# Expert blocks of 1024 columns, with tiles of the two experts in groups of four

## The chip, the cores and the metric

The kernel runs on one core of one Trainium2 chip. The core has a matrix engine (TensorE, PE in the rows, with its weight loads as PEld), a vector engine (VectorE, DVE), a scalar engine (ScalarE, ACT), GpSimd (POOL), and a synchronisation engine (SyncE, SP) that issues nearly all transfers here. Data comes from HBM by 16 DMA engines into SBUF; matrix products land in PSUM, which has eight banks of 512 float32 columns per partition. The metric is device time in microseconds, the median of three runs; a profile is one execution of the same program.

## The reference

Two decoder layers over 256 tokens of width 1024, all in float32. Each has a mixing part and a channel part. The channel part of layer 0 is a dense SwiGLU; that of layer 1, about which this document is, sends each token to two of eight experts:

```python
def _swiglu(x, w1, w3, w2):
    return (jax.nn.silu(x @ w1) * (x @ w3)) @ w2

logits = (xt @ w_router).astype(jnp.float32)
top_v, top_e = lax.top_k(logits, TOP_K)          # 2 of 8
gates = jax.nn.softmax(top_v, axis=-1)
...
y = jnp.zeros((T, D), x.dtype).at[stok].add(yb[dest] * sg[:, None].astype(x.dtype))
```

An expert has `w1` and `w3` of 1024 x 3584 and `w2` of 3584 x 1024, 44 MB of float32 in the three. All eight are read: 352 MB.

## The kernel before

Products in float32 are made from parts. ScalarE rounds a weight tile to a high part (`whi`, `cast_hi`, L1133), VectorE subtracts it from the raw tile to get the low part (`wlo`, `cast_lo`, L1141), and TensorE multiplies the parts in its fast format.

**Pairs of experts.** Experts are ranked by their load and worked on in four pairs. The first of a pair (role 0, "large" here) has up to 128 tokens, and each of its products takes three matmuls (`mm3`, L119 to L121). The second (role 1, "small") has at most 64 tokens, so that the high and the low parts of its tokens lie side by side in one stationary operand, and two matmuls do (`two`, L1080 and L1081); the halves are added later. Tokens are gathered by a matmul with a selection matrix (`select`, `gather`), one eighth of the width at a time, into `g`.

**Tiles and steps.** Work goes in steps, one for each weight tile of 1 MB (128 partitions x 2048 float32). `plan` lists them. The hidden width of 3584 is cut into blocks of `BN` = 512 columns, seven for each expert. A block has four up steps, two for `w1` and two for `w3`, each of four chunks of 128 rows by 512 columns; a row piece that the DMA reads is 2 KB. Then come the down steps of the block two before (the same expert's one before): two tiles of `w2`, each of two chunks of 128 rows with the full width of 1024, 4 KB in a row. Blocks of the two experts alternate, so that six steps of the large one are followed by six of the small one. A pair has 84 steps, the stage 336.

**What a block's result goes through.** The sums of a block gather in a PSUM bank (`mps`), one for `w1` and one for `w3`. For a large block `gated` takes the silu on ScalarE and `product` (L1258) multiplies on VectorE into `mh`; four transposes (`turn_pe`, `htp`, L1271) turn it, and `turn_large` splits it into `hi` and `lo`. For a small block `lift` (L1250) copies both sums to SBUF, matmuls with `fold` turn them and add the halves (`ftp`, L1267), and `turn_silu`, `turn_mult` (`fs`), `turn_small` (`sh`) follow. Down steps accumulate in two banks of each expert (`macc`). After an expert's last down step `sel_t` turns its selection matrix, `acc_split` splits its sum into `yh` and `yl`, and `combine` adds it to the tokens in four parts (`cbp`, then an add on VectorE into `x`, L1319).

**What sets the order.** `run` writes the order of every engine out by hand: at step s it first does what is noted in `mid[s]`, then casts the high part of step s + `ah` and the low part of step s + `al` (one less than the buffers of each, so both 4), asks for one more raw tile, does the step's matmuls, and then what is noted in `end[s]`. SP issues one transfer for each raw tile (`fetch`, L95) as soon as its buffer, one of six, is free: that is after the subtraction of the tile that held it. There are five buffers of high parts and five of low parts. PSUM has four banks for `mps`, `htp`, `ftp`, `gps`, `stp` and `cbp` together (`mmp`), and four for `macc`.

```python
        for s, (kind, bi, mat, k0) in enumerate(steps):
            for f in mid[s]:
                f()
            self.cast_hi(s + ah)
            self.cast_lo(s + al)
            self.more()
```

## Time and profile before

| | |
|---|---|
| median of three runs | 1692.51 us (1691.47 to 1692.65) |
| the profiled execution's own time | 1691.51 us |
| its span, first to last instruction | 1689.7 us |
| share of the span busy: TensorE, VectorE, ScalarE, GpSimd | 96%, 82%, 68%, 3% |
| transfers of expert weights | 336 of 1024 KB, median 11.5 us from issue to landing |

The first of the 336 transfers is issued at 755.31 us, so the last 55% of the span is the expert stage. Busy shares are averages over stages that differ; a matmul's busy time overlaps the next one's. Idle time is put down to the semaphore that came last.

### The profile page before, as it was taken

The page shows a single profiled execution, that of the slowest core. Times are in us where ns is not written, and L with a number is a line of the kernel's source. Part 1 is how long each engine was busy: PE and PEld are TensorE (multiplying, and loading weights), DVE is VectorE, ACT ScalarE, POOL GpSimd, SP SyncE. Part 2 cuts the span into 40 slices and gives each one's busy share as a digit, 9 for nine tenths or more (in the row PEclk, how much of TensorE's full clock was granted, in tenths as well). Part 3 has the DMA queues.
Part 4 walks back from the last instruction along what each step waited for, and adds up shares of the span by engine and source line. Part 5 has one row for each costly group of instructions (what it writes and reads, how often), then busy time and mean ns, then how long its engine had stood idle before and what let it go on. Part 6 is the DMA issues. An engine that isn't in the chain of part 4 may idle for free.

```text
span 1689.7 us, 22227 instructions
## 1 busy us (share of the span) xinstructions
PE 1625.3 (96%) x8152; PEld 1341.3 (79%) x8152; DVE 1386.1 (82%) x1686; ACT 1145.0 (68%) x1366; POOL 44.4 (3%) x40
## 2 busy tenths in 40 slices
PE   8899999999989999999999999999999999999996
PEld 7788787888878887877887787877878878778774
DVE  6987786554567667869999999999999998899987
ACT  5546744443436667448888888788887888778874
POOL 0331000000000000000000000000000000000000
PEclk9999999999999999999999999999999999999998
DMA  7534365555546443629999999999999999999993
GB/s 250 167 125 138 132 207 182 197 186 175 193 124 213 132 156 132 211 93 381 395 392 395 394 392 394 394 393 395 393 392 392 392 395 394 394 391 393 395 395 129
DMA packets 220733, 481.23 MB, mean 285 GB/s; under 512 B 8876, under 2 KB 33592, under 8 KB 220616
## 3 DMA queue, kind: packets, MB, share of 16 engines
q1 hardware_dynamic: 219272, 474.98, 77.3%
q0 software_dynamic: 1344, 4.75, 0.9%
q8 instruction: 66, 1.08, 0.3%
q14 instruction: 51, 0.42, 0.1%
HBM read 478.65 MB, written 1.05 MB: 284 GB/s over the span
## 4 chain that ended last, share of the span: by engine, by line
DMA 28%; DVE 15%; PE 6%; ACT 6%; issue 5%; ACTq 0%; DVEq 0%
DMA raw<-in_expert_w_dram 28%; DVE wlo L1141 11%; ACT whi L1133 5%; DVE x L1319 1%; PE plps L119 0%; PE plps L120 0%; PE plps L121 0%; PE bap L121 0%; PE bap L120 0%; PE yo L121 0%; PE bap L119 0%; PE yo L119 0%; PE yo L120 0%; DVE yl L128 0%; DVE mh L1258 0%
## 5 line engine op out<-in xcount | busy, mean ns | idle before, releaser
L1141 DVE TENSOR_TENSOR wlo<-raw,whi 128x2048 fp32r<-128x2048 f32 (+1 forms) x338 | 763.7, 2274 | 61.9 <-ACT whi L1133 59.9
L1133 ACT CAST whi<-raw 128x2048 fp32r<-128x2048 f32 (+1 forms) x338 | 641.3, 1902 | 152.9 <-DMA raw<-in_expert_w_dram 143.9
L107 DVE TENSOR_TENSOR wlo<-raw,whi 128x1024 fp32r<-128x1024 f32 (+2 forms) x218 | 254.7, 1190 | 148.1 <-issue 78.2
L105 ACT CAST whi<-raw 128x1024 fp32r<-128x1024 f32 (+2 forms) x222 | 218.5, 1016 | 177.5 <-PE hps L121 51.7
L119 PE MATMUL mps<-wlo,g 128*128 128x512 f32 x448 | 179.2, 400 | 1.8 <-DVE fs L1280 1.8
L1080 PE MATMUL mps<-wlo,g 128*128 128x512 f32 x448 | 179.8, 401 | 0.0
L1081 PE MATMUL mps<-whi,g 128*128 128x512 f32 x448 | 176.8, 395 | 0.0
L121 PE MATMUL mps<-whi,g 128*128 128x512 f32 x448 | 176.5, 394 | 0.0
L120 PE MATMUL mps<-whi,g 128*128 128x512 f32 x448 | 176.0, 393 | 0.0
L119 PEld LDWEIGHTS mps<-wlo,g 128*128 128x128 f32 x448 | 84.3, 188 | 20.5 <-DVE fs L1280 2.8
L121 PEld LDWEIGHTS mps<-whi,g 128*128 128x128 f32 x448 | 84.1, 188 | 19.4
L1080 PEld LDWEIGHTS mps<-wlo,g 128*128 128x128 f32 x448 | 84.8, 189 | 18.0
L1081 PEld LDWEIGHTS mps<-whi,g 128*128 128x128 f32 x448 | 84.9, 190 | 17.7
L120 PEld LDWEIGHTS mps<-whi,g 128*128 128x128 f32 x448 | 84.3, 188 | 17.9
L402 PE MATMUL dqp<-x,whi 128*128 128x512 f32 x256 | 95.5, 413 | 2.2 <-DVE vm L486 2.2
L1080 PE MATMUL macc<-wlo,sh 128*128 128x512 f32 x224 | 90.1, 402 | 3.0 <-DVE wlo L1141 1.8
L119 PE MATMUL macc<-wlo,hi 128*128 128x512 f32 x224 | 88.6, 396 | 0.0
L121 PE MATMUL macc<-whi,lo 128*128 128x512 f32 x224 | 88.2, 394 | 0.0
L120 PE MATMUL macc<-whi,hi 128*128 128x512 f32 x224 | 88.0, 393 | 0.0
L1081 PE MATMUL macc<-whi,sh 128*128 128x512 f32 x224 | 87.9, 393 | 0.0
L119 PE MATMUL hps<-wlo,x 128*128 128x512 f32 (+1 forms) x192 | 71.8, 374 | 0.0
L121 PE MATMUL hps<-whi,x 128*128 128x512 f32 (+1 forms) x192 | 71.4, 372 | 0.0
(373 smaller groups left out, 2958.7 us busy)
## 6 DMA issues: line engine op xcount, KB each, us to landing
raw<-in_expert_w_dram SPq DMA_DIRECT2D x336, 1024.0 KB, 11.5
raw<-in_w_in_dram SPq DMA_DIRECT2D x40, 1024.0 KB, 5.1
raw<-in_dense_w_dram SPq DMA_DIRECT2D x33, 1024.0 KB, 5.1
raw<-in_w_branch_diff_dram SPq DMA_DIRECT2D x8, 1024.0 KB, 5.0
raw<-in_w_out_dram SPq DMA_DIRECT2D x8, 1024.0 KB, 5.0
raw<-in_w_ple_gate_dram SPq DMA_DIRECT2D x8, 1024.0 KB, 5.1
raw<-in_w_branch_mla_dram SPq DMA_DIRECT2D x4, 1024.0 KB, 5.1
raw<-in_w_in_dram SPq DMA_DIRECT2D x4, 768.0 KB, 4.8
```

The source lines that it names most:

```text
L105: self.latest = nc.scalar.copy(hi[:, s], raw[:, s])
L107: nc.vector.tensor_tensor(lo[:, s], raw[:, s], hi[:, s], op=OP.subtract)
L119: mm(ps, sh, ml, start=first, stop=False)
L120: mm(ps, sh, mh, start=False, stop=False)
L121: mm(ps, sl, mh, start=False, stop=last)
L402: mm(*one, start=k == 0 and m == 0, stop=end and m == 1)
L1080: mm(ps, st, ml, start=first, stop=False)
L1081: mm(ps, st, mh, start=False, stop=last)
L1133: self.nc.scalar.copy(hi[:, p], raw[:, p])
L1141: self.nc.vector.tensor_tensor(lo[:, p], raw[:, p], self.his[s][:, p], op=OP.subtract)
L1319: nc.vector.scalar_tensor_tensor(self.x[:, tb, cs], ps, gate, self.x[:, tb, cs], op0=OP.mult, op1=OP.add, **kw)
```

## The change

`BN` becomes 1024. An expert has three blocks of 1024 columns and one of 512. An up tile of a wide block has two chunks of 128 rows by 1024 columns, 4 KB in a row; one of the last block stays as it was. A wide block has eight up steps and four down steps. `plan` no longer alternates whole blocks: four tiles of `w1` of the large expert, four of the small one, four of `w3` of each, then the four down tiles of the small block before and the four of the large block before.

A wide block uses two PSUM banks for each of `w1` and `w3`. The turn of a wide large block stands three steps after its last up step (two before); the turn of a small block stands after the last down step of the small block before it. Gathers for the next pair stand beside down steps, one at a time but for the last two. The combine of a small expert stands at one step, that of a large one at four. The low parts have four buffers instead of five (`al` is 3), `mh` has four instead of three, and the selection matrix is kept for two pairs instead of four. The number of matmuls and of casts is the same.

```diff
@@ -40,9 +40,9 @@
 HI_BUFS, XHI_BUFS = 3, 2
-LO_BUFS, XLO_BUFS = 2, 3
-MH_BUFS = 3
-BN = 512
+LO_BUFS, XLO_BUFS = 2, 2
+MH_BUFS = 4
+BN = 1024
 LCAP, SCAP = 128, 64
...
@@ -1081,14 +1081,16 @@
         mm(ps, st, mh, start=False, stop=last)
 
     def plan(self, jobs):
-        lanes, n = min(2, len(jobs)), EF // BN
-        blocks = [(m + a, i) for m in range(0, len(jobs), lanes) for i in range(n) for a in range(lanes)]
+        lanes, cuts = min(2, len(jobs)), range(0, EF, BN)
+        blocks = [(m + a, c0, min(BN, EF - c0)) for m in range(0, len(jobs), lanes) for c0 in cuts for a in range(lanes)]
         steps = []
-        for b in range(len(blocks) + lanes):
-            if b < len(blocks):
-                steps += [("up", b, mat, k0) for mat in (0, 1) for k0 in range(0, KC, 4)]
-            if b >= lanes:
-                steps += [("down", b - lanes, 0, r) for r in range(0, BN // 128, 2)]
+        for b0 in range(0, len(blocks) + lanes, lanes):
+            for mat in (0, 1):
+                for b in range(b0, min(b0 + lanes, len(blocks))):
+                    steps += [("up", b, mat, k0) for k0 in range(0, KC, 2048 // blocks[b][2])]
+            late = list(range(max(0, b0 - lanes), b0))
+            for b in late if b0 >= len(blocks) else late[::-1]:
+                steps += [("down", b, 0, r) for r in range(0, blocks[b][2] // 128, 2)]
         return blocks, steps
...
@@ -1104,15 +1106,15 @@
         if kind == "up":
-            nm, r, nk, c0, n = ("expert_w1", "expert_w3")[mat], k0, 4, i * BN, BN
+            nm, r, nk = ("expert_w1", "expert_w3")[mat], k0, 2048 // n
         else:
-            nm, r, nk, c0, n = "expert_w2", i * (BN // 128) + k0, 2, 0, D
+            nm, r, nk, c0, n = "expert_w2", c0 // 128 + k0, 2, 0, D
         w = self.i[nm][self.j][bass.ds(self.expert[m], 1), r * 128:(r + nk) * 128, c0:c0 + n]
...
@@ -1155,29 +1157,35 @@
+        lanes = 2 if pairs else 1
...
+        def after(b0):
+            return last["up", b0 + lanes - 1, 1] + 1
+
         for q in order[1:]:
             m = [x for x, job in enumerate(jobs) if job[0] == q][0]
-            s0 = first["up", blocks.index((m - 2, EF // BN - 1)), 0]
-            mid[s0 - 8].append(lambda q=q: self.select(q))
-            mid[s0].append(lambda q=q: new_g(q))
-            for x, d in enumerate((0, 1, 2, 3, 6, 7, 8, 9)):
-                end[s0 + d].append(lambda q=q, x=x: self.gather(gs[q], q, (x,), wide, self.mmp, "mm"))
-
-        for bi, (m, i) in enumerate(blocks):
+            b0 = [x for x, blk in enumerate(blocks) if blk[0] == m - 2][2]
+            mid[first["up", b0, 0]].append(lambda q=q: self.select(q))
+            mid[after(b0)].append(lambda q=q: new_g(q))
+            for x, d in enumerate((0, 1, 2, 4, 5, 6, 7, 7)):
+                end[after(b0) + d].append(lambda q=q, x=x: self.gather(gs[q], q, (x,), wide, self.mmp, "mm"))
+
+        for bi, (m, c0, n) in enumerate(blocks):
             small = jobs[m][2]
             s1, s3 = last["up", bi, 0], last["up", bi, 1]
             if small:
                 for mat, s in ((0, s1), (1, s3)):
                     mid[s + 1].append(lambda bi=bi, mat=mat: self.lift(ups, hid, bi, mat))
+                t = last["down", bi - lanes, 0] if bi >= lanes else s3 + 2
             else:
                 mid[s1 + 1].append(lambda bi=bi: self.gated(ups, hid, bi))
                 mid[s3 + 1].append(lambda bi=bi: self.product(ups, hid, bi))
-            t = s3 + 2
+                t = s3 + n // 512 + (1 if n > 512 else 0)
             end[t].append(lambda bi=bi: self.turn_pe(hid, turn, bi))
...
@@ -1185,22 +1193,30 @@
-            if i == EF // BN - 1:
+            if c0 + n == EF:
                 d0, d1 = first["down", bi, 0], last["down", bi, 0]
-                over = m == len(jobs) - 1
-                near = m >= len(jobs) - 2
-                end[d0].append(lambda m=m: self.sel_t(accs, m))
-                if over:
+
+                def parts(*at):
+                    for part, s in enumerate(at):
+                        end[s].append(lambda m=m, part=part: self.combine(accs, m, (part,), None))
+
+                if m == len(jobs) - 1:
+                    end[d0].append(lambda m=m: self.sel_t(accs, m))
                     end[d1].append(lambda m=m: self.acc_split(accs, m))
                     end[d1].append(lambda m=m: self.combine(accs, m, range(4), done))
-                elif near:
+                elif m == len(jobs) - 2:
+                    end[d0].append(lambda m=m: self.sel_t(accs, m))
                     mid[d1 + 1].append(lambda m=m: self.acc_split(accs, m))
-                    end[d1 + 1].append(lambda m=m: self.combine(accs, m, range(4), None))
+                    parts(*[d1 + 1] * 4)
+                elif small:
+                    end[d0].append(lambda m=m: self.sel_t(accs, m))
+                    mid[d1 + 1].append(lambda m=m: self.acc_split(accs, m))
+                    parts(*[d1 + 2] * 4)
                 else:
-                    x, y = (d1 + 7, d1 + 13) if small else (d1 + 1, d1 + 7)
-                    mid[x].append(lambda m=m: self.acc_split(accs, m))
-                    for part in range(4):
-                        end[y + part].append(lambda m=m, part=part: self.combine(accs, m, (part,), None))
+                    z = after(bi + 4)
+                    end[z].append(lambda m=m: self.sel_t(accs, m))
+                    mid[z + 1].append(lambda m=m: self.acc_split(accs, m))
+                    parts(z + 2, z + 4, z + 5, z + 6)
...
@@ -1214,31 +1230,33 @@
             if kind == "up":
                 if k0 == 0:
-                    ups[bi, mat] = self.mmp.tile([128, 512], F32, name="mps", tag="mm")
-                for k in range(4):
-                    w = [t[:, k * BN:(k + 1) * BN] for t in (hi, lo)]
-                    ends = k0 + k == 0, k0 + k == KC - 1
-                    if small:
-                        self.two(ups[bi, mat], gs[q][:, k0 + k, 1], *w, *ends)
-                    else:
-                        self.mm3(ups[bi, mat], gs[q][:, k0 + k, 0], gs[q][:, k0 + k, 2], *w, *ends)
+                    ups[bi, mat] = [self.mmp.tile([128, 512], F32, name="mps", tag="mm") for _ in range(n // 512)]
+                for k in range(2048 // n):
...
@@ -1246,56 +1264,71 @@
...
     def gated(self, ups, hid, bi):
-        hid[bi] = h = self.hidden()
-        self.nc.scalar.activation(h, ups.pop((bi, 0)), AF.Silu)
+        hid[bi] = []
+        for ps in ups.pop((bi, 0)):
+            h = self.hidden()
+            self.nc.scalar.activation(h, ps, AF.Silu)
+            hid[bi].append(h)
 
     def product(self, ups, hid, bi):
-        self.nc.vector.tensor_tensor(hid[bi], hid[bi], ups.pop((bi, 1)), op=OP.mult)
+        for h, ps in zip(hid[bi], ups.pop((bi, 1))):
+            self.nc.vector.tensor_tensor(h, h, ps, op=OP.mult)
 
     def turn_pe(self, hid, turn, bi):
         nc = self.nc
+        small = self.jobs[self.blocks[bi][0]][2]
         hs = hid.pop(bi)
-        if self.jobs[self.blocks[bi][0]][2]:
-            ps = self.mmp.tile([128, 2, 4, SCAP], F32, name="ftp", tag="mm")
-            for a in range(2):
+        turn[bi] = {"ps": []}
+        for n in range(self.blocks[bi][2] // 512):
+            if small:
+                ps = self.mmp.tile([128, 2, 4, SCAP], F32, name="ftp", tag="mm")
+                for a in range(2):
+                    for q in range(4):
+                        nc.tensor.matmul(ps[:, a, q, :], hs[a][n][:, q * 128:(q + 1) * 128], self.fold, start=True, stop=True)
+            else:
+                ps = self.mmp.tile([128, 4, 128], F32, name="htp", tag="mm")
                 for q in range(4):
-                    nc.tensor.matmul(ps[:, a, q, :], hs[a][:, q * 128:(q + 1) * 128], self.fold, start=True, stop=True)
-        else:
-            ps = self.mmp.tile([128, 4, 128], F32, name="htp", tag="mm")
-            for q in range(4):
-                nc.tensor.transpose(ps[:, q, :], hs[:, q * 128:(q + 1) * 128], self.ident)
-        turn[bi] = {"ps": ps}
+                    nc.tensor.transpose(ps[:, q, :], hs[n][:, q * 128:(q + 1) * 128], self.ident)
+            turn[bi]["ps"].append(ps)
...
     def turn_large(self, turn, bi):
-        hh, hl = (self.mp.tile([128, 4, 128], F32R, name=nm) for nm in ("hi", "lo"))
-        self.split(hh, hl, turn[bi]["ps"])
+        hh, hl = (self.mp.tile([128, 2, 4, 128], F32R, name=nm, tag=nm, bufs=2) for nm in ("hi", "lo"))
+        for n, ps in enumerate(turn[bi]["ps"]):
+            self.split(hh[:, n], hl[:, n], ps)
         turn[bi] = {"st": (hh, hl)}
```

On VectorE, one round in the middle of the first pair, from one `product` (`mh<-mh,mps`) to the small split (`sh<-fs,sh`). Before, with its low parts (`wlo`) between:

```order
L1141 TENSOR_TENSOR wlo<-raw,whi 128x2048 x3
L1258 TENSOR_TENSOR mh<-mh,mps 128x512
L1141 TENSOR_TENSOR wlo<-raw,whi 128x2048 x2
L128 TENSOR_TENSOR lo<-htp,hi 128x512
L1141 TENSOR_TENSOR wlo<-raw,whi 128x2048 x6
L1280 TENSOR_TENSOR fs<-fs,ftp 128x256
L1141 TENSOR_TENSOR wlo<-raw,whi 128x2048
L128 TENSOR_TENSOR sh<-fs,sh 128x4x64
```

and now, on the same engine:

```order
L1143 TENSOR_TENSOR wlo<-raw,whi 128x2048 x9
L1283 TENSOR_TENSOR mh<-mh,mps 128x512 x2
L1143 TENSOR_TENSOR wlo<-raw,whi 128x2048 x3
L128 TENSOR_TENSOR lo<-htp,hi 128x512 x2
L1143 TENSOR_TENSOR wlo<-raw,whi 128x2048 x5
L1311 TENSOR_TENSOR fs<-fs,ftp 128x256 x2
L1143 TENSOR_TENSOR wlo<-raw,whi 128x2048
L128 TENSOR_TENSOR sh<-fs,sh 128x4x64 x2
```

The instructions between low parts now come by twos, half as often, and three low parts instead of two stand between a product and the split of its turned form.

On TensorE, the turn of a small block (`ftp`). Before, it stood between a small down tile (`macc<-whi,sh`) and the large expert's next up tile:

```order
L1080 MATMUL macc<-wlo,sh 128x512
L1081 MATMUL macc<-whi,sh 128x512
L1267 MATMUL ftp<-fold,mh 128x64 x8
L119 MATMUL mps<-wlo,g 128x512
L120 MATMUL mps<-whi,g 128x512
L121 MATMUL mps<-whi,g 128x512
```

and now it stands between the small and the large down tiles:

```order
L1080 MATMUL macc<-wlo,sh 128x512
L1081 MATMUL macc<-whi,sh 128x512
L1295 MATMUL ftp<-fold,mh 128x64 x16
L119 MATMUL macc<-wlo,hi 128x512
L120 MATMUL macc<-whi,hi 128x512
L121 MATMUL macc<-whi,lo 128x512
```

Two turns now stand together, and four large down tiles come behind them, with four large up tiles after those.

On TensorE, the turn of a large block (`htp`). Before, behind two large down tiles:

```order
L119 MATMUL macc<-wlo,hi 128x512
L120 MATMUL macc<-whi,hi 128x512
L121 MATMUL macc<-whi,lo 128x512
L1271 MATMUL htp<-ident,mh 128x128 x4
L1080 MATMUL mps<-wlo,g 128x512
L1081 MATMUL mps<-whi,g 128x512
```

and now behind the third small up tile:

```order
L1080 MATMUL mps<-wlo,g 128x512
L1081 MATMUL mps<-whi,g 128x512
L1299 MATMUL htp<-ident,mh 128x128 x8
L1080 MATMUL mps<-wlo,g 128x512
L1081 MATMUL mps<-whi,g 128x512
```

The two turns of a wide block stand inside a group of small up tiles, whose fourth tile follows them.

## Rows read from the trace of the kernel before

**Rows 1.** The page: busy time of each engine, and GB/s in 40 slices.

```profile
span 1689.7 us, 22227 instructions
...
PE 1625.3 (96%) x8152; PEld 1341.3 (79%) x8152; DVE 1386.1 (82%) x1686; ACT 1145.0 (68%) x1366; POOL 44.4 (3%) x40
...
GB/s 250 167 125 138 132 207 182 197 186 175 193 124 213 132 156 132 211 93 381 395 392 395 394 392 394 394 393 395 393 392 392 392 395 394 394 391 393 395 395 129
```

**Rows 2.** The page: the chain that ended last, by engine and by line.

```profile
DMA 28%; DVE 15%; PE 6%; ACT 6%; issue 5%; ACTq 0%; DVEq 0%
DMA raw<-in_expert_w_dram 28%; DVE wlo L1141 11%; ACT whi L1133 5%; DVE x L1319 1%; PE plps L119 0%; PE plps L120 0%; PE plps L121 0%; PE bap L121 0%; PE bap L120 0%; PE yo L121 0%; PE bap L119 0%; PE yo L119 0%; PE yo L120 0%; DVE yl L128 0%; DVE mh L1258 0%
```

**Rows 3.** Busy time by stretch: engines with counts, clock, DMA share, GB/s.

```profile
1084.00:1307.00 223.00, 218.47 (x1027) 178.43 (x1026) 209.00 (x128) 182.49 (x147) 0.00 (x0) 1.00 1.04 393
...
1020.00:1080.00 60.00, 58.54 (x267) 47.00 (x265) 58.68 (x41) 48.67 (x36) 0.00 (x0) 1.00 1.04 393
```

**Rows 4.** ScalarE in order of time: start, duration, casts that waited for a landing.

```profile
1105.53 1.92 ACT L1133 CAST whi<-raw 128x2048 fp32r<-128x2048 f32 x1 [0.33 <-DMA raw<-in_expert_w_dram]
...
1113.67 1.91 ACT L1133 CAST whi<-raw 128x2048 fp32r<-128x2048 f32 x1 [0.83 <-DMA raw<-in_expert_w_dram]
...
1118.87 1.91 ACT L1133 CAST whi<-raw 128x2048 fp32r<-128x2048 f32 x1 [0.19 <-DMA raw<-in_expert_w_dram]
...
1121.56 1.92 ACT L1133 CAST whi<-raw 128x2048 fp32r<-128x2048 f32 x1 [0.29 <-DMA raw<-in_expert_w_dram]
...
1129.55 1.91 ACT L1133 CAST whi<-raw 128x2048 fp32r<-128x2048 f32 x1 [0.70 <-DMA raw<-in_expert_w_dram]
...
1134.75 1.91 ACT L1133 CAST whi<-raw 128x2048 fp32r<-128x2048 f32 x1 [0.74 <-DMA raw<-in_expert_w_dram]
...
1137.43 1.90 ACT L1133 CAST whi<-raw 128x2048 fp32r<-128x2048 f32 x1 [0.29 <-DMA raw<-in_expert_w_dram]
```

**Rows 5.** Busy time by stretch: down tiles, up tiles, then down tiles alone.

```profile
1113.50:1118.60 5.10, 5.10 (x23) 4.12 (x23) 4.66 (x4) 4.42 (x4) 0.00 (x0) 1.00 1.03 398
1118.60:1129.30 10.70, 10.09 (x45) 7.90 (x44) 9.88 (x7) 8.21 (x6) 0.00 (x0) 1.00 1.05 391
...
1647.00:1655.00 8.00, 7.98 (x35) 6.19 (x34) 7.45 (x5) 6.94 (x6) 0.00 (x0) 1.00 1.03 410
```

**Rows 6.** The chain in order of time: start, duration, what.

```profile
1043.35 8.92 DMA raw<-in_expert_w_dram
...
1112.52 11.65 DMA raw<-in_expert_w_dram
...
1655.57 1.92 ACT whi L1133
```

**Rows 7.** The page: issues, count, KB of one, median us from issue to landing.

```profile
raw<-in_expert_w_dram SPq DMA_DIRECT2D x336, 1024.0 KB, 11.5
raw<-in_w_in_dram SPq DMA_DIRECT2D x40, 1024.0 KB, 5.1
```

**Rows 8.** Groups, 1084 to 1307 us: busy, mean ns, idle before and its end.

```profile
L1141 DVE TENSOR_TENSOR wlo<-raw,whi 128x2048 fp32r<-128x2048 f32 x84 | 190.9, 2286 | 14.5 <-ACT whi L1133 13.8 <-PE macc L1081 0.4
...
L119 PE MATMUL mps<-wlo,g 128*128 128x512 f32 x110 | 44.1, 401 | 0.8 <-DVE fs L1280 0.8
...
L1267 PE MATMUL ftp<-fold,mh 128*128 128x64 f32 x112 | 13.9, 273 | 1.1 <-ACT mh L1250 1.1
...
L1271 PE MATMUL htp<-ident,mh 128*128 128x128 f32 x28 | 4.4, 278 | 2.1 <-DVE mh L1258 2.0
```

**Rows 9.** TensorE in order of time: first starts of two blocks, a small turn.

```profile
772.57 0.41 PE L119 MATMUL mps<-wlo,g 128*128 128x512 f32 x1
...
783.64 0.39 PE L1080 MATMUL mps<-wlo,g 128*128 128x512 f32 x1
...
1013.26 1.89 PE L1267 MATMUL ftp<-fold,mh 128*128 128x64 f32 x16
1014.97 0.48 PE L119 MATMUL mps<-wlo,g 128*128 128x512 f32 x1
```

More of the change, by code (lines that the diff above doesn't have):

```diff
@@ L958, in before_moe @@
         self.places(cps, m, gg, eq)
-        self.sel = rp.tile([128, 2, NP, 256], F32R, name="sel", tag="sel")
+        self.sel = rp.tile([128, 2, 2, 256], F32R, name="sel")
         self.select(0)
@@ L1106, in more @@
         kind, bi, mat, k0 = self.steps[t]
[L1107 removed]
+        m, c0, n = self.blocks[bi]
         if m not in self.expert:
@@ L1216, in run @@
             self.more()
-            m, i = blocks[bi]
+            m, c0, n = blocks[bi]
             q, role, small = jobs[m]
@@ L1278, in turn_mult @@
+    def turn_silu(self, turn, bi):
+        turn[bi]["s"] = []
+        for ps in turn[bi]["ps"]:
+            s = self.mp.tile([128, 4, SCAP], F32, name="fs", bufs=2)
+            self.nc.scalar.activation(s, ps[:, 0], AF.Silu)
+            turn[bi]["s"].append(s)
     def turn_mult(self, turn, bi):
-        s = turn[bi]["s"]
-        self.nc.vector.tensor_tensor(s, s, turn[bi]["ps"][:, 1], op=OP.mult)
+        for s, ps in zip(turn[bi]["s"], turn[bi]["ps"]):
+            self.nc.vector.tensor_tensor(s, s, ps[:, 1], op=OP.mult)
@@ L1282, in turn_small @@
     def turn_small(self, turn, bi):
-        hh = self.mp.tile([128, 4, 128], F32R, name="sh")
-        self.split(hh[:, :, :SCAP], hh[:, :, SCAP:], turn[bi]["s"])
+        hh = self.mp.tile([128, 2, 4, 128], F32R, name="sh")
+        for n, s in enumerate(turn[bi]["s"]):
+            self.split(hh[:, n, :, :SCAP], hh[:, n, :, SCAP:], s)
         turn[bi] = {"st": (hh,)}
     def turn_large(self, turn, bi):
-        hh, hl = (self.mp.tile([128, 4, 128], F32R, name=nm) for nm in ("hi", "lo"))
-        self.split(hh, hl, turn[bi]["ps"])
+        hh, hl = (self.mp.tile([128, 2, 4, 128], F32R, name=nm, tag=nm, bufs=2) for nm in ("hi", "lo"))
@@ L1293, in sel_t @@
         q, _, small = self.jobs[m]
-        st = accs[m]["st"] = self.mp.tile([128, T], F32R, name="selt", bufs=2)
+        st = accs[m]["st"] = self.mp.tile([128, T], F32R, name="selt")
         ps = self.mmp.tile([128, 512], F32, name="stp", tag="mm")
```

38 lines of the change are left out of this document (23 added, 15 removed).

## The prediction

> **What bounds the kernel now.** The page's busy shares come first: TensorE 96% of the span, VectorE 82%, and a GB/s line that jumps from about 150 to 394 near slice 18 and stays there to the end [rows 1]. Shares over the span cannot say who ends last, so the chain of waits comes next. Its largest part by far is the transfer of expert weights, 28% of the span, ahead of the low-part subtraction on VectorE at 11% [rows 2]. One pair of experts is 84 tiles of 1 MB; the stretch from 1084 to 1307 us holds 84 subtractions [rows 8], so it is one pair's worth of work. In it the DMA moves 393 GB/s at a share of 1.04 while VectorE is busy 209.0 and ScalarE 182.5 of 223 us [rows 3]. TensorE looks full at 218.5, but a matmul's busy time overlaps the next one's, so I count it by starts further down. In the timeline of ScalarE, almost every cast starts when a tile lands [rows 4]: the queue is never empty and the engines wait for it. So the expert stage, which is where the whole change lies, lasts as long as its 336 tiles take to land.
>
> **What a row's width is worth.** A tile's cost can be read from the distance of two landings. Six tiles in the old order are four up tiles (rows of 2 KB) and two down tiles (rows of 4 KB). The cast that starts at 1105.53 is followed by the one six tiles later at 1121.56 and by the next at 1137.43: 16.03 and 15.87 us, 15.95 on the mean, 223.3 for 84 tiles [rows 4]. The two down tiles inside them take 1118.87 - 1113.67 = 5.20 and 1134.75 - 1129.55 = 5.20 us, 2.60 each [rows 4]; where only down tiles are left, from 1647 to 1655 us, the rate is 410 GB/s, or 1.0486 MB / 410 = 2.56 us each [rows 5]. The up tiles are what is left: (15.95 - 5.20) / 4 = 2.69 us, or 2.71 with 2.56 for a down tile. Short stretches say the same in GB/s: 398 over a stretch of down tiles, 391 over one of up tiles [rows 5].
>
> The change gives 4 KB rows to three of the three and a half blocks of each expert: 24 of its 28 up tiles, 192 of 224 in all; the last half block keeps 2 KB. Each gains between 2.69 - 2.60 = 0.09 and 2.71 - 2.56 = 0.15 us, so 192 tiles gain 17 to 29 us. I take 2.70 and 2.58, 0.12 us a tile, **-23 us**. The time of 84 tiles falls from 223.3 to 223.3 - 48 x 0.12 = 217.5 us.
>
> The Trainium skill (DMA: Bandwidth & Descriptors, Why small descriptors are slow) speaks for less: it gives a fixed overhead of about three cycles per packet beside 32-byte beats, so 2 x 67 = 134 cycles for two 2 KB packets and 131 for one of 4 KB, 2.2%, which would be 0.06 us a tile and 11.5 us in all, an estimate from that page. The trace, with 2.70 against 2.58, shows about twice that, and the measured landings decide the sum.
>
> **Who comes next.** TensorE: 48 matmuls of 512 columns start between 772.57 and 783.64 us, 0.2306 us each [rows 9]. A tile of the first expert (role 0, called large here) takes 12 of them, 2.77 us; of the second (small) 8, 1.84 us. A pair has 42 x 12 + 42 x 8 = 840, and 16 more combine results: 856 x 0.2306 = 197.4. To this come seven turns of small blocks at 1014.97 - 1013.26 = 1.71 us [rows 9], 12.0; seven turns of large ones, 4.4 at most [rows 8]; and 32 gather matmuls of 192 columns, 2.8 (an estimate by their columns from the same 0.2306). Together 216.6 us, against 217.5 for the new transfers. The change alters none of these counts. So the second bound stands 0.9 us behind the first, and every wait of TensorE that isn't already inside a wait for data now costs time. In the pair shown, the waits with a name are 0.8 for the small block's product, 1.1 for its lifted halves, and 2.1 for the product ahead of a large turn [rows 8]. If all 4.0 stayed, a pair would take 220.6 and the loss would be 4 x 3.1 = 12; if none did, 0. The causes of the last two are weakened: the rows of the order show that the turn of a large block now stands three small tiles behind the product instead of two tiles, the product stands behind the low parts of one tile fewer (three ahead instead of four, as there is one buffer less), and the small turn is now behind the four down tiles after its last lift, not two. So I take a value nearer to the lower end, **+5 us** (0 to 12).
>
> VectorE needs at most its 209.0 busy us of a pair [rows 3], 8.5 less than 217.5; its instructions are the same in number, and that margin hides the two adds or subtractions that now stand together, and the four adds of a combine at one step. ScalarE has 35 us to spare. The smaller selection table, the larger hidden tiles and the fewer descriptors cost nothing behind the same margins. The start of the stage is unchanged ahead of the first landing. After the last landing, 34.1 us pass (cast at 1655.57, end of the span 1689.7) [rows 1, 6]; the same steps stand there but for a small turn that moves ahead, 2 us at best, and TensorE may arrive 4 us later. I count **0** (-2 to +4).
>
> **Sum.** The profiled execution took 1691.5 by its own time, 1689.7 of it the span. 1691.5 - 23 + 5 + 0 = 1673.5. The median of the runs is 1.0 above that execution, so I forecast **1674.5 us**. Its own range, from the bounds, is 1692.5 - 29 - 2 = 1661.5 to 1692.5 - 17 + 12 + 4 = 1691.5; I hold 1666 to 1681 as its likely part.
>
> **Rivals.**
>
> *Half the gain, because rows are far apart.* A down tile is one contiguous megabyte, an up tile's rows lie 14,336 bytes apart (3584 columns of 4 bytes); no row of before shows wide rows with such gaps. If they land halfway, at 2.64 us, the gain is 11.5; 84 tiles then take 220.4, TensorE has 3.8 spare and the +5 goes away: 1692.5 - 11.5 = 1681. By the packet rule of the Trainium skill (DMA: Bandwidth & Descriptors, Why small descriptors are slow) the time would be the same.
>
> *TensorE becomes the bound.* All waits with a name stay and the bunched combine adds its own: 1692.5 - 23 + 12 = 1681.5, up to 1689 if each pair loses 2 us more. For it: 0.9 us of room. Against it: the order of the turns.
>
> *Nothing moves.* If wide rows with gaps land like narrow ones (2.70), the same transfers bound the stage: 1692.5.
>
> *Slower: the swing no longer fits in the buffers.* In the old order TensorE is late by a small turn, six large tiles and a large turn against six landings: 1.71 + 16.6 + 0.4 - 15.95 = 2.8 us, given back over six small tiles. In the new one, two small turns, four large down tiles and four large up tiles stand together: 3.4 + 22.1 - 8 x 2.58 = 4.9 us late, and 6.6 with five gathers of 0.35 us between, which three of the fourteen rounds have; there are four buffers for the low part instead of five. If none of the lateness could be carried, each round of 24 tiles would lose about 4.9 + 11.1 - 10.3 = 5.7 us, 80 over 14 rounds; half of that gives 1692.5 - 23 + 40 = 1709. It decides where (23 + 3.4) / 14 = 1.9 us a round are lost. Against it: a tile now waits 11.5 us from issue to landing, while the same size takes 5.1 us on a queue with little in it [rows 7], so some 6.4 us of lateness fit before the queue runs dry; at 1043 us the wait had shrunk to 8.92 from 11.65 [rows 6] and the rate stayed at 393 [rows 3].
>
> **How the numbers follow.** The forecast's part, 1666 to 1681, 46%; half the gain 13%; TensorE's waits 16%; better than 1666, 4%; nothing 10%; slower 11%. A change of 0.2%, 3.4 us, is about what a measurement of this kernel can tell from none: faster means under 1689.1, slower over 1695.9. Faster 0.46 + 0.13 + 0.16 + 0.04 = 0.79, same 0.10, slower 0.11. The range reaches from 1665, near the best case, to 1691, past the two cases of a smaller gain, and leaves out about 2 in 10.
>
> **What the next profile would show.** Right: GB/s in the stage near 405 instead of 394, distances of landings near 2.58 us for wide up tiles, the chain still through the transfers, issue to landing swinging between 6 and 12 us, and waits of TensorE at the turns below the 1.1 and 2.1 us a pair. Half the gain: 398 to 400 GB/s with landings still in the chain. TensorE's bound: a rate under 403 with dips, and a chain through matmuls and low parts. Slower: slices under 380 GB/s and TensorE idle behind small groups. The forecast falls if wide rows with gaps land above 2.65 us, or if TensorE idles more than 3 us a pair beyond its waits for data.

## The result, and the profile after

The changed kernel takes 1671.15 us (median of four runs, 1670.91 to 1671.95), the kernel before 1692.58 us (four runs, 1691.47 to 1693.17): a ratio of 0.9878, 95% interval 0.9865 to 0.9891, 21.4 us less. The forecast was 1674.5 with a range of 1665 to 1691. The profiled execution took 1670.91 by its own time, 1669.1 of it the span; the span before was 1689.7 [rows 1], so 20.6 us of the difference are inside it.

The page of the changed kernel, to be read against [rows 1] and [rows 7]:

```profile
span 1669.1 us, 22506 instructions
...
PE 1617.4 (97%) x8152; PEld 1343.1 (80%) x8152; DVE 1380.3 (83%) x1686; ACT 1137.4 (68%) x1366; POOL 43.5 (3%) x40
...
GB/s 242 180 117 125 157 186 174 211 186 179 182 122 223 137 156 139 195 109 304 400 401 409 398 409 409 403 403 397 408 409 401 403 403 404 409 404 408 406 397 129
...
raw<-in_expert_w_dram SPq DMA_DIRECT2D x336, 1024.0 KB, 9.5
```

The GB/s line rises from a flat 391 to 395 in the expert stage to 397 to 409. A tile now waits 9.5 us from issue to landing instead of 11.5, so there is less in the queue ahead of it. Engine counts are the same to the instruction, so nothing was saved by doing less. The same 223 us as in [rows 3], by stretch:

```profile
1084.00:1307.00 223.00, 222.45 (x1070) 184.19 (x1069) 213.05 (x132) 184.88 (x151) 0.00 (x0) 1.00 1.03 404
```

TensorE starts 1070 matmuls where it started 1027, and is idle for 0.55 us instead of 4.5. Its waits from 800 to 1630 us (line, tile, what it waited for, sum, times, longest) are now these three and no more:

```profile
PE mps L119 <- DVE x L1352: 3.5, 3, 1.5
PE mps L119 <- DVE lo L128: 3.3, 1, 3.3
PE stp L1331 <- DVE lo L128: 1.1, 1, 1.1
```

The waits ahead of the turns, 1.1 and 2.1 us in one pair before [rows 8], do not occur in this stretch. What stands beside the transfers as a bound can be seen in one view. ScalarE in order of time (start, duration, tile, and in brackets the idle time before it and what ended it):

```profile
1190.87 1.90 ACT L1135 CAST whi<-raw 128x2048 fp32r<-128x2048 f32 x1 [0.56 <-DMA raw<-in_expert_w_dram]
...
1195.99 1.91 ACT L1135 CAST whi<-raw 128x2048 fp32r<-128x2048 f32 x1 [0.38 <-DMA raw<-in_expert_w_dram]
1198.58 1.91 ACT L1135 CAST whi<-raw 128x2048 fp32r<-128x2048 f32 x1 [0.68 <-PE macc L121]
1201.37 1.91 ACT L1135 CAST whi<-raw 128x2048 fp32r<-128x2048 f32 x1 [0.89 <-PE macc L121]
1204.17 1.91 ACT L1135 CAST whi<-raw 128x2048 fp32r<-128x2048 f32 x1 [0.89 <-PE macc L121]
1206.97 1.91 ACT L1135 CAST whi<-raw 128x2048 fp32r<-128x2048 f32 x1 [0.89 <-PE mps L121]
```

Up to 1195.99 casts start when a tile lands, like those of [rows 4]. Then TensorE comes to the large tiles; from 1198.58 on each cast waits for a matmul to give a buffer back, and they stand 2.79 us apart, the length of twelve matmuls. The bound changes hands inside the round. Over the whole stretch from 800 to 1630 us the casts wait about as long for the matmuls of the large expert (L121) as for landings:

```profile
ACT whi L1135 <- DMA raw<-in_expert_w_dram: 52.8, 87, 1.8
ACT whi L1135 <- PE mps L121: 43.4, 44, 3.9
ACT whi L1135 <- PE macc L121: 17.3, 16, 1.4
```

The page's chain could be followed back here over the last 11% of the span only ("PE 10%; DVE 1%"), so it says little by itself; no transfer stands in that part.

Where the 20.6 us lie: the first expert matmul and the cast of the last whole tile, to be read against 772.57 [rows 9] and 1655.57 [rows 6].

```profile
774.85 0.42 PE L119 MATMUL mps<-wlo,g 128*128 128x512 f32 x1
```

```profile
1634.40 1.92 ACT L1135 CAST whi<-raw 128x2048 fp32r<-128x2048 f32 x1 [0.36 <-DMA raw<-in_expert_w_dram]
```

Between the two marks 883.0 us became 859.55: -23.4. Ahead of them the stage begins 2.3 us later, behind them the span goes on for 34.7 us instead of 34.1: +0.6. Together -20.5, the span's difference but for rounding.

### The profile page after: what moved, and what is told of

Same layout as the page of the kernel before. It is cut to its first block, busy times and chain, and to the rows that moved or that the text cites. A ratio compares the mean times of both kernels' runs of the same rounds, so it can differ in the third digit from the quotient of the medians.

```text
span 1669.1 us, 22506 instructions
## 1 busy us (share of the span) xinstructions
PE 1617.4 (97%) x8152; PEld 1343.1 (80%) x8152; DVE 1380.3 (83%) x1686; ACT 1137.4 (68%) x1366; POOL 43.5 (3%) x40
## 5 line engine op out<-in xcount | busy, mean ns | idle before, releaser
L1143 DVE TENSOR_TENSOR wlo<-raw,whi 128x2048 fp32r<-128x2048 f32 (+1 forms) x338 | 753.4, 2272 | 29.2 <-ACT whi L1135 20.5
L119 PE MATMUL mps<-wlo,g 128*128 128x512 f32 x448 | 177.8, 397 | 6.8 <-DVE x L1352 3.5
L1080 PE MATMUL mps<-wlo,g 128*128 128x512 f32 x448 | 177.4, 396 | 0.0
L121 PE MATMUL mps<-whi,g 128*128 128x512 f32 x448 | 177.3, 396 | 0.0
L121 PEld LDWEIGHTS mps<-whi,g 128*128 128x128 f32 x448 | 84.4, 188 | 20.2
L121 PE MATMUL macc<-whi,lo 128*128 128x512 f32 x224 | 88.3, 394 | 0.0
L121 PE MATMUL hps<-whi,x 128*128 128x512 f32 (+1 forms) x192 | 71.3, 372 | 0.0
```

Of the source, the lines that this page charges most:

```text
L119: mm(ps, sh, ml, start=first, stop=False)
L121: mm(ps, sl, mh, start=False, stop=last)
L1080: mm(ps, st, ml, start=first, stop=False)
L1143: self.nc.vector.tensor_tensor(lo[:, p], raw[:, p], self.his[s][:, p], op=OP.subtract)
```

## The experiments

Twelve kernels ran. Each is compared with the kernel before on the same chip (1691.6 to 1692.0 there); gains beside the changed kernel are differences to its 1671.15. Beside that the kernel before stood at 1692.58, so about 1 us of such a difference can come from place and time alone. Where it matters, a stretch inside the trace is given too: from the cast of the first expert tile to that of the last whole one, both started by landings, 871.38 us in the changed kernel and 894.79 before (760.78 to 1655.57). In the first two, theory A has the gain come from the width of the rows, theory B from the order; the later ones ask what bounds the two kernels, and each names its own cases.

**1. The new order with narrow rows.** Up tiles of the wide blocks hold four chunks of 512 columns; the order of tiles by expert and kind is that of the changed kernel.

```diff
         if kind == "up":
             nm, r, nk = ("expert_w1", "expert_w3")[mat], k0, 2048 // n
+            if n == 1024:
+                c, r, nk, n = k0 // 4, k0 % 4 * 2, 4, 512
+                c0 += c * 512
```

Expected:

> The order, the blocks and the groups of the changed kernel, but an up tile of a wide block is read as four chunks of 128 rows by 512 columns, 2 KB in a row. Theory A (the rows' width made the transfers faster, and the transfers bounded the stage): landings of up tiles return to about 2.70 us, the rate to 394 GB/s, and the time to 1688 to 1694 us. Theory B (the order of groups and turns took waits from TensorE, and the width only came with it): the time stays within 1671 to 1677 us.

Measured: 1693.36 us, ratio 1.0015 (1.0003 to 1.0027). All of the gain is gone. Its stretch over one run of wide-block tiles:

```profile
1202.00:1242.00 40.00, 40.00 (x175) 32.32 (x174) 34.19 (x16) 30.21 (x20) 0.00 (x0) 1.00 1.05 387
```

and the same blocks, then down tiles, then the last half blocks (still 2 KB rows) in the changed kernel:

```profile
1194.00:1230.00 36.00, 36.00 (x157) 29.23 (x156) 33.54 (x18) 28.93 (x20) 0.00 (x0) 1.00 1.03 408
1068.00:1085.00 17.00, 17.00 (x80) 13.90 (x79) 17.00 (x13) 15.88 (x15) 0.00 (x0) 1.00 1.03 410
1152.00:1170.00 18.00, 18.00 (x89) 14.99 (x88) 14.46 (x9) 14.03 (x18) 0.00 (x0) 1.00 1.05 389
```

Rows of 4 KB that lie 14,336 bytes apart move at 408 GB/s, a contiguous tile at 410, rows of 2 KB at 387 to 389. So the gaps cost next to nothing and the width is everything: the first rival (half the gain) falls.

**2. Wide rows with the old order.** The plan of before, block by block, with blocks of 1024 columns. Groups of one expert are therefore twice as long as before.

```diff
-        for b0 in range(0, len(blocks) + lanes, lanes):
...
+        for b in range(len(blocks) + lanes):
+            if b < len(blocks):
+                steps += [("up", b, mat, k0) for mat in (0, 1) for k0 in range(0, KC, 2048 // blocks[b][2])]
+            if b >= lanes:
+                steps += [("down", b - lanes, 0, r) for r in range(0, blocks[b - lanes][2] // 128, 2)]
...
+                    parts(d1 + 2, d1 + 4, d1 + 5, d1 + 6)
```

Expected:

> Blocks of 1024 columns with 4 KB rows as in the changed kernel, but the steps in the old order: all up tiles of a block, then the down tiles of the same expert's block before, and the combine of a large expert right behind its last down step. Theory A: wide up tiles land in 2.56 us, and TensorE, late by up to 7 us behind twelve large tiles, costs a little: 1671 to 1680 us. Theory B: without the new order the gain is lost: 1685 us or more.

Measured: 1683.54 us, ratio 0.9955 (0.9943 to 0.9966), between what the two theories gave. Its page shows the rate falling in some slices (369, 357, 377), and its waits of TensorE from 800 to 1650 us are others:

```profile
PE cbp L1345 <- DVE x L1349: 6.4, 6, 1.5
PE cbp L1345 <- DVE lo L128: 3.2, 2, 2.5
PE mps L1080 <- ACT mh L1267: 2.4, 3, 0.8
```

With narrow rows the new order gains nothing over the plan of before (1693.36, experiment 1). With wide rows it is 12.4 us better than this plan, but here the groups of one expert are twelve tiles long, twice those of before, so the two comparisons are not of the same step; wide rows with groups of six were not run. What the long groups cost is seen at the queue: the shortest time from issue to landing is 4.7 us, against 5.9 in the changed kernel, so the queue runs dry in places, as in experiment 12.

**3 and 4. A lighter TensorE.** Both kernels leave out the third matmul (low part of the activations) of the large expert's up and down products, 168 of 856 matmuls a pair, 39 us: experiment 3 in the changed kernel, experiment 4 in the kernel before.

```diff
-                        self.mm3(ups[bi, mat][c], gs[q][:, k0 + k, 0], gs[q][:, k0 + k, 2], *w, *ends)
+                        self.two(ups[bi, mat][c], gs[q][:, k0 + k, 0], *w, *ends)
```

Expected of 3:

> The changed kernel without the third matmul (the low part of the tokens) of the large expert's up and down steps, so TensorE has some 39 us less to do for a pair; this part of the products is left out. If TensorE now bounds the stage (216.6 us a pair against 215 of transfers), the time falls by 8 to 14 us, to 1657 to 1663, with landings all at 2.56 us and the chain through the transfers. If the transfers or VectorE bound it, it stays within 3 us of 1671.

Expected of 4:

> The kernel before without the same third matmul of the large expert's steps; that part of the products is left out. If the transfers bound that kernel, its stage does not move, and the time falls only by what TensorE is late at the end: 1686 to 1692 us. If TensorE's waits bound it, the time falls by 10 us or more.

Measured: experiment 4 takes 1692.81 us, ratio 1.0008 (0.9993 to 1.0022). TensorE only waits more (from 800 to 1630 us):

```profile
PE htp L1271 <- DVE mh L1258: 89.6, 26, 5.2
```

So TensorE did not bound before; that its transfers did is shown together with experiment 1, where the rows' width alone undoes the gain.

Experiment 3 takes 1665.91 us, 5.2 less than the changed kernel, between its two cases (8 to 14 less, or within 3 us). In it the casts mostly chase the landings; two casts thirteen wide tiles apart, each started by a landing:

```profile
1198.58 1.91 ACT L1135 CAST whi<-raw 128x2048 fp32r<-128x2048 f32 x1 [0.64 <-DMA raw<-in_expert_w_dram]
...
1231.81 1.92 ACT L1135 CAST whi<-raw 128x2048 fp32r<-128x2048 f32 x1 [0.65 <-DMA raw<-in_expert_w_dram]
```

33.23 us over 13 distances is 2.56 us a wide tile, where 2.58 was forecast. Where the 5.2 us lie is told by the casts of the first and the last whole expert tile, of the changed kernel first (its last one stands above) and then of experiment 3:

```profile
763.02 1.91 ACT L1135 CAST whi<-raw 128x2048 fp32r<-128x2048 f32 x1 [1.57 <-DMA raw<-in_expert_w_dram]
```

```profile
760.98 1.92 ACT L1135 CAST whi<-raw 128x2048 fp32r<-128x2048 f32 x1 [1.25 <-DMA raw<-in_expert_w_dram]
...
1631.81 1.92 ACT L1135 CAST whi<-raw 128x2048 fp32r<-128x2048 f32 x1 [0.36 <-DMA raw<-in_expert_w_dram]
```

The stage's landings take 870.83 us here and 871.38 in the changed kernel. Of the 5.5 us between the two spans, 2.0 lie ahead of the first cast and 2.9 behind the last one, where fewer matmuls are left to do; the 39 us a pair less of TensorE shorten the landings by 0.6 us in all. So TensorE alone does not hold the changed kernel back either: for the stage the expectation's second case holds. Something else keeps the landings above the 857 us that these 333 distances need at 2.56 and 2.70 us; before was above its own sum too, 894.79 against 885. One such place can be seen behind the end of the first pair, where the four adds of the small expert's combine stand at one step. TensorE waits for them, and the cast that needs a weight buffer from TensorE waits in its turn:

```profile
1036.07 0.50 PE L1080 MATMUL mps<-wlo,g 128*128 128x512 f32 x1 [3.39 <-DVE x L1352]
```

```profile
1039.73 5.82 ACT L1135 CAST whi<-raw 128x2048 fp32r<-128x2048 f32 x3 [4.29 <-PE mps L1081]
```

**5. Groups that alternate without a break.**

```diff
-            for b in late if b0 >= len(blocks) else late[::-1]:
+            for b in late:
```

Expected:

> The changed kernel, with the down tiles of a round in the order large, small instead of small, large, so that the groups of four alternate without a break (in the changed kernel eight small and then eight large tiles follow each other across the seam: small up, small down, then large down, large up). Against the changed kernel's 1671.2 us. Theory A (transfers and TensorE are tied, 2.56 us a wide tile against 0.23 us a matmul, and the buffers already carry the swing of about 5 us): the swing gets smaller but nothing was lost to it, 1669 to 1673 unless a turn now waits. Theory B (the swing of eight large tiles is what TensorE and the transfers lose the last 10 us to, since the stage lasts 877 us where its landings alone need about 867): 1663 to 1668. A third possibility: the turn of the small block comes later and the large downs, now first, wait for the large block's turn, which shows as a wait of the accumulating matmuls (macc) for hi or lo, 0.5 to 1.5 us a round, 1678 to 1692.

Measured: 1674.36 us, ratio 0.9900 (0.9884 to 0.9916), 3.2 more than the changed kernel and outside all three. The wait that grows is not at the turn, where the third possibility put it, but at the combine (800 to 1630 us):

```profile
PE cbp L1348 <- DVE x L1352: 5.7, 3, 2.6
```

The waits of TensorE with a name rise by 1.2 us in all, from 7.9 to 9.1; the rest of the 3.2 is not explained.

**6. The small expert's combine spread out.**

```diff
-                    parts(*[d1 + 2] * 4)
+                    parts(d1 + 2, d1 + 4, d1 + 6, d1 + 8)
```

Expected:

> The changed kernel, with the four parts of the small expert's combine at four steps two apart instead of all at one. Three waits of the up matmuls for the adds into x (3.5 us in all after 800 us) should go from the trace. Theory A (transfers and TensorE tied; a wait of 1.2 us at three places is given back out of the buffers): the waits go, the time moves by less than 1.5 us, 1669.5 to 1672. Theory B (TensorE is the only bound, each wait with a name costs its length): -3.5 us, 1667 to 1668.5.

Measured: 1669.56 us, ratio 0.9869 (0.9854 to 0.9885), 1.6 less. TensorE's waits:

```profile
PE mps L119 <- DVE lo L128: 2.7, 1, 2.7
PE stp L1331 <- DVE lo L128: 1.9, 2, 1.4
PE mps L1080 <- DVE x L1352: 1.4, 3, 0.6
```

Their sum fell from 7.9 to 6.0 us, 1.9, the time by 1.6 and the stretch of landings by 1.75 (1632.67 - 763.04 = 869.63 us). The three agree, but the size is not clear of noise: the intervals of the two ratios overlap, and the same stretch is 1.6 us longer than the changed kernel's in experiment 7, which changes nothing in the stage. The edit also took away only 2.1 of the 3.5 us, so the two theories are not told apart.

**7. The stretch ahead of the experts at its old place.**

```diff
-                with pool("pre") as n.mp, tc.manual_schedule():
+                with pool("pad") as dp, pool("pre") as n.mp, tc.manual_schedule():
+                    tc.nc.gpsimd.memset(dp.tile([128, 3072], F32, name="pad")[:, :1], 0.0)
```

Expected:

> The changed kernel, with 12 KB per partition left unused below the tiles of the stretch ahead of the experts, so that these lie where they lay before the change (the smaller selection table and the missing low-part buffer had moved them down by 4 + 8 KB). Theory A (the cast of the router weights waits 2.9 us for a matmul of the previous layer because its tile now lies on a tile which that matmul still reads; the wait is there only through the placement): the wait goes, the first expert issue comes 1.3 us earlier, 1669.5 to 1670.3. Theory B (the later start is only the drift between two runs, or another cause): the first issue stays at 757 to 758 and the time at 1671 to 1672.

Measured: 1669.37 us, with a wider scatter (1666.03 to 1672.74; ratio 0.9869, 0.9851 to 0.9887). The row of the changed kernel, and the same row here:

```profile
737.26 0.25 ACT L127 CAST rwh<-rw 128x64 fp32r<-128x64 f32 x1 [2.94 <-PE prps L121]
```

```profile
732.96 0.23 ACT L127 CAST rwh<-rw 128x64 fp32r<-128x64 f32 x1
```

The wait of 2.94 us is in every kernel with the new placement and in none with the old one: the placement causes it. How much it costs at the end stays open within 1 to 2 us, as the runs of this kernel scatter by more. The start of the first expert matmul does not settle it: 772.25 to 774.89 us in the nine kernels with the wait and 768.69 to 773.89 in the five without, 2.1 us earlier on the mean, in one execution of each.

**8. Rows of 8 KB for the down tiles.** Each partition takes two rows that follow each other, and the turns read the hidden columns with a stride of two.

```diff
+        rows = "o (k p) n -> p (o k) n" if kind == "up" else "o (p k) n -> p (o k) n"
...
-                    nc.tensor.transpose(ps[:, q, :], hs[n][:, q * 128:(q + 1) * 128], self.ident)
+                    nc.tensor.transpose(ps[:, q, :], hs[n][:, q // 2 * 256 + q % 2:(q // 2 + 1) * 256:2], self.ident)
```

Expected:

> The changed kernel, with rows of 8 KB for the down tiles: each partition takes two rows of expert_w2 that follow each other, and the turns pick the hidden columns with a stride of two. Width is the cause under test, doubled once more for 112 of 336 tiles. Theory A (a cost per packet, which halving the packets from 2 KB to 4 KB brought from 2.70 to 2.56 us a tile, so another halving brings 0.07): down tiles land 2.49 us apart, the transfers need 8 us less, and because TensorE needs 216 us a pair the kernel gains only what waits TensorE sheds, 1667 to 1671. Theory B (4 KB rows already land at the ceiling of about 410 GB/s): down tiles stay at 2.56, 1670 to 1672. Against both: if the strided columns slow the turns on TensorE, 1672 to 1676, and the rows of htp and ftp get longer.

Measured: 1671.06 us, ratio 0.9882 (0.9866 to 0.9898): the same as the changed kernel. The stretch of landings is the same too, 871.82 us:

```profile
761.57 1.91 ACT L1136 CAST whi<-raw 128x2048 fp32r<-128x2048 f32 x1 [1.55 <-DMA raw<-in_expert_w_dram]
...
1633.39 1.91 ACT L1136 CAST whi<-raw 128x2048 fp32r<-128x2048 f32 x1 [0.29 <-DMA raw<-in_expert_w_dram]
```

But the edit also makes TensorE's turns longer, as the expectation's third case had it. The two small turns of a wide block up to the next matmul, in the changed kernel and here:

```profile
1026.32 3.68 PE L1295 MATMUL ftp<-fold,mh 128*128 128x64 f32 x32
1029.81 0.48 PE L119 MATMUL macc<-wlo,hi 128*128 128x512 f32 x1
```

```profile
1025.33 3.87 PE L1296 MATMUL ftp<-fold,mh 128*128 128x64 f32 x32
1029.01 0.48 PE L119 MATMUL macc<-wlo,hi 128*128 128x512 f32 x1
```

They take 3.68 us instead of 3.49, and two large turns 0.86 instead of 0.79. Over the stage's fourteen rounds that is 3.6 us more for TensorE, an estimate.

**9. The same rows with the lighter TensorE.** The edits of experiments 8 and 3 in one kernel, which leaves out what experiment 3 does.

Expected:

> The changed kernel with rows of 8 KB for the down tiles, and without the third matmul (low part of the activations) of the large expert's up and down products, which takes about 39 us a pair from TensorE; beside the same cut with 4 KB rows, 1665.9. Theory A (with TensorE light, the transfers of 865 us bound the stage, and wider rows take 8 us off them): 1656 to 1660. Theory B (with TensorE light, VectorE with its 95 busy us of 100 bounds the stage next, and the transfers only follow): 1663 to 1666, with landings that stand farther apart than the 2.49 and 2.56 us of one tile on an undisturbed queue.

Measured: 1658.38 us, ratio 0.9799 (0.9775 to 0.9823), 7.5 less than experiment 3, where the doubled rows were expected to take 8 off the transfers. Two casts ended by landings, six down tiles apart:

```profile
1172.38 1.90 ACT L1136 CAST whi<-raw 128x2048 fp32r<-128x2048 f32 x1 [0.62 <-DMA raw<-in_expert_w_dram]
...
1187.32 1.91 ACT L1136 CAST whi<-raw 128x2048 fp32r<-128x2048 f32 x1 [0.61 <-DMA raw<-in_expert_w_dram]
```

14.94 / 6 = 2.49 us a tile. The time lies in theory A's range, though the runs scatter from 1652.19 to 1661.04 us. The stretch of landings:

```profile
762.73 1.92 ACT L1136 CAST whi<-raw 128x2048 fp32r<-128x2048 f32 x1 [1.34 <-DMA raw<-in_expert_w_dram]
...
1627.45 1.92 ACT L1136 CAST whi<-raw 128x2048 fp32r<-128x2048 f32 x1 [0.30 <-DMA raw<-in_expert_w_dram]
```

It takes 864.72 us. With the three others this makes a square: 871.4 us in the changed kernel, 870.8 with TensorE lighter (experiment 3), 871.8 with wider rows (experiment 8), 864.7 with both. Either alone moves it by less than 1 us and both together by 6.7: transfers and TensorE are nearly tied in the changed kernel. How nearly is open within some 4 us, since each stretch is of one execution and experiment 8's turns give TensorE 3.6 us more to do.

**10 and 11. The edits together.** Experiment 10 puts 6, 7 and 8 into one kernel, experiment 11 only 6 and 7.

Expected of 10:

> Three edits on the changed kernel together: rows of 8 KB for the down tiles, the small expert's combine spread over four steps, and the tiles ahead of the experts at their old place. Against the changed kernel's 1671.2 us. Theory A (TensorE is the bound of the expert stage now, with about 868 us of starts one behind the other and 8 us of gaps; transfers stand behind it): the edits that touch TensorE's gaps and the start add up, -1.6 and -1.8, and the rows add nothing, 1667 to 1669. Theory B (transfers and TensorE are tied, so that only both together give the full gain): the rows' 8 us of transfers come on top in part, 1660 to 1666.

Expected of 11:

> The changed kernel with the small expert's combine spread over four steps and the tiles ahead of the experts at their old place, rows of the down tiles 4 KB as in the changed kernel. It stands beside the run that has the 8 KB rows too. Theory A (TensorE is the bound): the same time as with the 8 KB rows within 1.5 us, 1667 to 1669. Theory B (tied): 1667 to 1669 here, and at least 2 us more than with the 8 KB rows.

Measured: 1668.99 us (1666.53 to 1670.57; ratio 0.9877, 0.9861 to 0.9894) with the wider rows, 1666.21 us (1662.77 to 1668.68; ratio 0.9855, 0.9834 to 0.9877) without. The wider rows add nothing; with them the kernel is 2.8 us slower, more than the 1.5 us that theory A allowed, which fits the longer turns of experiment 8. This does not tell TensorE as the only bound from a tie, since the rows' edit itself gives TensorE more to do. Experiment 11 is the fastest whole kernel, some 5 us below the changed kernel by the medians and 0.8 below what both theories gave; the intervals of the two ratios overlap. In its profiled execution (1666.49 us) 3.5 of the 4.4 us lie ahead of the first expert matmul (771.38 against 774.85).

**12. Five raw tiles instead of six.**

```diff
-RAW_BUFS = 4
+RAW_BUFS = 3
```

Expected:

> The changed kernel with five tiles in flight for the raw weights instead of six. It tries the slower rival at its edge: how much of the swing of large and small groups the queue carries. In the changed kernel a tile takes 5.9 to 11.6 us from issue to landing. Theory A (4.9 to 6.6 us of lateness a round fit only just into six tiles): with five, some 2.6 us less fit, the queue runs dry in the rounds with a large swing, 0.5 to 1.5 us a round are lost, 1676 to 1692, and the shortest time from issue to landing falls to about 5 us, that of a lone tile. Theory B (the low parts and the highs that lie ahead of TensorE carry the swing, and the raw tiles only part of it): 1671 to 1674.

Measured: 1695.46 us, ratio 1.0031 (1.0018 to 1.0044): slower than the kernel before. From its page:

```profile
GB/s 240 151 124 138 139 205 188 194 185 187 193 122 191 147 150 142 217 123 357 362 403 404 397 408 370 396 384 390 409 401 381 380 391 406 406 371 372 395 392 134
...
raw<-in_expert_w_dram SPq DMA_DIRECT2D x336, 1024.0 KB, 8.1
```

and what its casts waited for from 800 to 1630 us:

```profile
ACT whi L1135 <- DMA raw<-in_expert_w_dram: 100.0, 153, 2.2
```

The rate falls to 370 to 384 in places, the casts wait 100.0 us for landings (52.8 in the changed kernel), the shortest time from issue to landing falls from 5.9 to 5.0 us, as theory A said, and the 24.3 us more than in the changed kernel are 1.7 us for each of the fourteen rounds, a little more than theory A's upper end.

## Why the prediction was right, point by point

**The bound before.** Right, and now shown: 39 us less of TensorE a pair changed nothing (experiment 4), and rows of 2 KB in the new order give back the whole gain (experiment 1).

**The width, -23 us.** Right in its mechanism, too small in size. A wide tile lands in 2.56 us and a narrow one in 2.70, a gain of 0.14 instead of 0.12; 84 tiles need 48 x 2.56 + 8 x 2.70 + 28 x 2.56 = 216.2 us instead of 223.3, so the term was -28.4, near the forecast's upper bound of 29. I had taken 2.58, the middle between two readings of a contiguous down tile (2.60 and 2.56); rows with gaps land like the faster of the two.

The Trainium skill (DMA: Bandwidth & Descriptors, Why small descriptors are slow) puts a fixed overhead of about three cycles on each packet beside its 32-byte beats. By that, an estimate, two packets of 4 KB against one of 8 KB take 262 to 259 cycles, 1.2%, or 0.03 us a tile. The same section of the Trainium skill names a second fixed part, 32 bytes of descriptor metadata for each DMA operation; counted as one more beat a packet, the estimate becomes 264 to 260 cycles, 0.04 us. The trace disagrees in size for both steps: 0.14 us from 2 to 4 KB and 0.07 us from 4 to 8 KB (experiments 3 and 9). Halving the packets of a tile from 512 to 256 and from 256 to 128 saved in the ratio of two to one, as a fixed cost per packet does; it is only about twice as large as these estimates.

**TensorE as second bound, 216.6 against 217.5, +5 us.** The near tie was foreseen and is there, though with transfers at 216.2 neither of the two stands clearly first: experiments 3, 8 and 9 show that each alone moves the landings by less than 1 us and both together by 6.7. The price of +5 matched in number, but by luck. -28.4 for the transfers and -23.4 measured between the two marks leave +5.0; with TensorE lighter 4.4 of these remain (870.83 - 894.79 = -24.0), so at most 0.6 is the price of TensorE's length. The prediction had the price come from waits at the turns; none occur. What it hid behind VectorE's margin, the four adds of a combine at one step, is a cost instead: TensorE waits 3.5 us for them in the changed kernel and 10.1 in experiment 3. How much of the 4.4 that makes up is open; spreading them gave 1.6 us, which is not clear of noise (experiment 6). So the second rival, at 1681.5, did not come true.

**The start, 0.** It was +2.3 us between the two profiled executions. The change makes the selection table and the low-part buffers smaller, tiles below move, and the cast of one of them now waits 2.94 us for a matmul of the earlier layer (experiment 7). I had listed the smaller table under what costs nothing, which is wrong for this wait; how much of the 2.3 us it makes is not shown, as the start moves by up to 5 us among kernels of the same placement.

**The tail, 0.** Right: +0.6. **Sum by the steps:** 1691.5 - 28.4 + 5.0 + 2.3 + 0.6 = 1671.0, against 1670.9 for the profiled execution. The sum has to close, as +5.0 is a remainder; it shows where the time lies, not why. Against the forecast the width brought 5.4 us more, and start and tail took 2.9 back, so that the forecast missed by 3.4 only is partly luck.

**The signs.** Right were the rate (404), the landings, the swing of issue to landing (5.9 to 11.6 us) and the vanished waits at the turns. The rate does not tell the bounds apart, though: it is 404 from 800 to 1600 us in the changed kernel and with the lighter TensorE of experiment 3 alike. Wrong was the chain through the transfers: where it can be followed further than in the changed kernel, in experiment 6, the page has it mostly through TensorE:

```profile
PE 50%; DMA 4%; DVE 3%; ACT 1%; issue 0%; ACTq 0%; DVEq 0%; SPq 0%
```

**The slower rival.** It did not happen, but was nearer than the 11% make it look: one tile in flight less and it decides (experiment 12). The 6.4 us of room that the prediction read out of 11.5 against 5.1 us were just enough for a swing of 4.9 to 6.6; with 2.6 us less of it the whole gain is lost. That five raw tiles cost this much was measured; that the four low-part buffers lost nothing beside five was not tried, since there is no room for five beside the larger hidden tiles.

## What to carry to other kernels

Price a wider row by the distance of two landings of one tile in the trace, then ask at once which engine stands behind the transfers, and by how much: here the row was worth 28 us, of which 23 were had. Where two bounds are nearly tied, making one lighter shows little, and only both together tell; compare a stretch inside the trace, as a whole kernel's time also holds its start and its end. The order gave nothing with narrow rows, and groups twice as long cost 12 us with wide ones, so width and order must be tried together. Making a buffer smaller moves its neighbours, and a moved tile can take on a wait that no line of the diff shows.

## What the runs showed of the hardware that was not expected

Rows of 4 KB with gaps of 10 KB between them moved at 408 GB/s, contiguous tiles at 410. Rows of 8 KB still landed faster than rows of 4 KB, 2.49 against 2.56 us a megabyte, about 421 GB/s, so 4 KB was not yet the ceiling. Reading hidden columns with a stride of two made the turns longer on TensorE, 3.68 us instead of 3.49 for 32 matmuls of 64 columns, which the time of experiment 8 does not show.
